# A pace per step for the modulation dots, weights of the seven-product stage split a step ahead

## The chip, the cores and the metric

The kernel runs on one core of a Trainium2 chip. The metric is the device time of one execution in microseconds (us); the time of a kernel is the median of its runs. One execution is also recorded by the hardware profiler, and every row below comes from that one record.

## What is computed

A two-layer encoder over two sequences of 512 tokens (here s0 and s1), width 1024, all in fp32. Layer 0 mixes tokens by bidirectional retention (4 heads), layer 1 by grouped-query attention. Both layers have a squared-ReLU MLP of inner width 4096, and both norms of a layer are modulated: six vectors of 1024 per layer and sequence come from one matrix-vector product with the conditioning vector `c`.

```python
def adaln(c, w, b):
    mod = jax.nn.silu(c) @ w + b            # w: 1024 x 6144
    return [m[:, None, :] for m in jnp.split(mod, 6, axis=-1)]
...
for i in range(DEPTH):
    sh1, sc1, g1, sh2, sc2, g2 = adaln(c, mod_w[i], mod_b[i])
    h = rmsnorm(x, norm1_g[i]) * (1.0 + sc1) + sh1
    m = retention(h, ...) if i % 2 == 0 else attention(h, ...)
    x = x + g1 * m
    h = rmsnorm(x, norm2_g[i]) * (1.0 + sc2) + sh2
    x = x + g2 * (jnp.square(jax.nn.relu(h @ w1)) @ w2)
return rmsnorm(x, final_g)
```

## The kernel before

**Matmuls.** Activations are kept transposed, as eight tiles of 128 features by 512 tokens per sequence. Each fp32 operand is split into a high part (a copy rounded by ACT) and a low part (the difference, taken by DVE), and each product is three matmuls of 128x128 by 128x512 (`mm3`, the lines L220, L221, L222). A weight of the mixers comes as one `raw` tile of 128x1024 on SP's queue; `load_piece` splits it into `whi` (ACT, L207) and `wlo` (DVE, L208). One such piece feeds 24 matmuls.

**Stages in order of time.** The head (to 43 us); retention in eight steps, one head of one sequence each (s0 in steps 0 to 3, s1 in steps 4 to 7, to about 927 us); the entry of the MLP stage of layer 0, with s0's last up projections (`ups`) before and after the pools are changed at about 952 us; its seven-product part (1024 to 1530); the last down projections; attention (1576 to 1985); the same MLP stage for layer 1; the final norm. A retention step runs `scores`, `v` (four pieces), `g` (one piece), `y`, an interleaved list of pieces for the next step's queries and keys and this step's other gates (`ORDER`), and `out`. Step 3 also carries the first norm of s1, step 7 the second norm of s0: the sum of squares is multiplied out on PE, a chain of small DVE operations on 128x4 values (L271, L237 to L244) takes the root, DVE lays it on a diagonal (L275), PE spreads that (`spread`, L281), and DVE and ACT modulate eight tiles (L290, L293; in the MLP stages L312, L315).

**Modulation as background work.** After the first chunks, the modulation product runs on DVE: one task reads a 128x1024 block of `modw`, as two tiles loaded from POOL's queue (L409), and makes two `dot` instructions (L384, an elementwise product with a running sum) for each sequence: four, or two where a chunk is for s1 only. `mod_chunk` queues eight tasks for each chunk. `tick` is called at every mixer piece, behind its `wlo`: it adds `pace[0]` to a credit, and when the credit reaches 1 it issues the dots of one task and asks for the loads of the next. So a pace above 1 still gives one task a piece, and the rest of the credit is kept. `bg_until` and `flush` issue tasks down to a count at given points. The tiles of a task come from the pool `f2`, where one pair is free beside the conditioning and rotary tables; a chunk with `alt` takes every second pair from the pool `xfp` instead, so that two tasks' loads can be under way. Without it one load is under way at a time.

**The seven-product stage.** `wide_stage` closes the mixer's pools and opens its own: `sf` (forms), `su` (sums), `sq` (raw weights `rawq` of 128x1024 and their split halves `wh`). It finishes s0's down projections, s1's norm and s1's first up and down projections with these tiles, each weight loaded, split (L227 on ACT, L228 on DVE) and used in one call, while `h_forms` and `h_fetch` build the activations' forms (DVE L732 to L735 and L228). Then `wide_mlp` multiplies two-by-two blocks by seven products (`seven`, L668 to L670). The forms of the hidden activations are parked in DRAM, fetched back from POOL's queue (`fetch_form`), and split by a `cut` (ACT L816, DVE). `after` queues a cut behind the fetch with a count of three products (`late`).

**What sets the order.** Each engine runs its own instructions in the order in which the scheduler puts them, which follows the program's order and its dependencies. A tile that takes the place of one that is still read waits for the reader, and a pool opened over closed ones waits for the tiles that lay there.

## Time and profile before

| | us |
|---|---|
| Median of 3 runs | 2625.1 (2623.26 to 2627.22) |
| Profiled execution | 2615.62 |
| Its span | 2613.8 |
| PE busy | 2518.2 (96%) |
| DVE busy | 1992.3 (76%) |
| ACT busy | 1119.3 (43%) |
| POOL busy | 522.2 (20%) |

PE is the engine that almost never rests; the other three are meant to feed it. The time that a change of order can give or take is therefore what PE lacks of its own steady pace, stall by stall: its idle time, and the stretches after an idle time in which its granted clock is the lower of the two levels.

### The profile page before, as it was taken

To read this page: it belongs to the slowest core of one execution; us is meant where nothing else is said; L and a number is where in the kernel's file an instruction comes from. 1 tells how busy PE (TensorE), PEld (TensorE's weight loads), DVE (VectorE), ACT (ScalarE), POOL (GpSimd) and SP (SyncE) were. 2 spreads that over 40 slices of the span, in tenths; PEclk is the share of its full clock that TensorE was granted. 3 is DMA by queue.
4 is the path that set the end of the run, shared out by engine and by line. 5 is a ranking of instruction groups with operands and counts; after the bars stand their busy time and mean duration, and the time that the engine had idled before them with its cause. 6 is when DMAs were issued, how large, how long until landed. Compare 5 with 4: busy or idle time off the path is not lost. (4 is left out here: it accounts for less than half of the span.)

```text
span 2613.8 us, 32647 instructions
## 1 busy us (share of the span) xinstructions
PE 2518.2 (96%) x11186; PEld 2052.8 (79%) x11186; DVE 1992.3 (76%) x3800; ACT 1119.3 (43%) x1949; POOL 522.2 (20%) x947
## 2 busy tenths in 40 slices
PE   6999998899999999999999999899999999999998
PEld 4878886677888787888788887688788788878887
DVE  7777687879889877676778876877767766688877
ACT  3433233223323444444533344776764444454432
POOL 2312212331221212221421110000114122142100
PEclk9999999999999999999999999999999999999999
DMA  7544445655455655544654444123257444475433
GB/s 251 188 152 147 156 146 163 200 168 165 142 169 162 196 163 196 173 148 159 225 185 131 145 138 125 57 65 94 93 157 275 159 158 161 149 270 164 140 95 105
DMA packets 133994, 414.00 MB, mean 158 GB/s; under 512 B 21250, under 2 KB 24194, under 8 KB 133828
## 3 DMA queue, kind: packets, MB, share of 16 engines
q0 software_dynamic: 68352, 224.58, 25.7%
q1 hardware_dynamic: 59284, 180.32, 22.1%
q10 hardware_dynamic: 6192, 7.02, 0.8%
q8 instruction: 88, 1.44, 0.2%
q14 instruction: 78, 0.64, 0.1%
HBM read 332.15 MB, written 79.69 MB: 158 GB/s over the span
## 5 line engine op out<-in xcount | busy, mean ns | idle before, releaser
L207 ACT ACTIVATE whi<-raw 128x1024 fp32r<-128x1024 f32 x174 | 183.8, 1058 | 332.2 <-PE pm L221 106.3
L220 PE MATMUL pm<-r,whi 128*128 128x512 f32 x768 | 304.2, 399 | 13.3 <-ACT r L1180 5.8
L221 PE MATMUL pm<-r,whi 128*128 128x512 f32 x768 | 302.9, 394 | 4.9 <-DVE r L315 2.4
L222 PE MATMUL pm<-r,wlo 128*128 128x512 f32 x768 | 301.2, 393 | 0.5 <-DVE wlo L208 0.5
L208 DVE TENSOR_TENSOR wlo<-raw,whi 128x1024 fp32r<-128x1024 f32 x174 | 214.6, 1234 | 94.3 <-ACT whi L207 93.7
L227 ACT ACTIVATE wh<-rawq 128x512 fp32r<-128x512 f32 x228 | 142.5, 629 | 291.8 <-PE pm L669 160.7
L227 ACT ACTIVATE wh<-sum 128x512 fp32r<-128x512 f32 x208 | 129.8, 629 | 280.0 <-PE pa L669 176.5
L668 PE MATMUL pa<-r,wh 128*128 128x512 f32 x624 | 242.8, 389 | 0.0
L670 PE MATMUL pa<-r,wh 128*128 128x512 f32 x624 | 242.8, 389 | 0.0
L669 PE MATMUL pa<-r,wh 128*128 128x512 f32 x624 | 242.7, 389 | 0.0
L384 DVE SCALAR_TENSOR_TENSOR junk<-f,f 128x512 bf16<-128x512 f32 x280 | 194.3, 694 | 52.1 <-DMA f<-in_modw_dram 49.2
L409 POOL DMA_DIRECT2D f<-in_modw_dram x168 | 90.7, 540 | 474.5 <-DVE junk L384 378.2
L220 PEld LDWEIGHTS pm<-r,whi 128*128 128x128 f32 x768 | 145.9, 190 | 48.3 <-ACT r L1180 6.2
L668 PE MATMUL pm<-r,wh 128*128 128x512 f32 x468 | 182.9, 391 | 0.9 <-ACT wh L227 0.9
L669 PE MATMUL pm<-r,wh 128*128 128x512 f32 x468 | 182.2, 389 | 0.0
L670 PE MATMUL pm<-r,wh 128*128 128x512 f32 x468 | 182.1, 389 | 0.0
L220 PE MATMUL pa<-whi,r 128*128 128x512 f32 x440 | 174.4, 399 | 5.5 <-ACT whi L207 4.2
L221 PEld LDWEIGHTS pm<-r,whi 128*128 128x128 f32 x768 | 146.3, 190 | 38.2 <-DVE r L293 4.3
L228 DVE TENSOR_TENSOR wh<-sum,wh 128x512 fp32r<-128x512 f32 x208 | 141.6, 686 | 44.9 <-ACT wh L227 43.4
L221 PE MATMUL pa<-wlo,r 128*128 128x512 f32 x440 | 174.8, 397 | 0.6 <-DVE wlo L208 0.6
L222 PE MATMUL pa<-whi,r 128*128 128x512 f32 x440 | 174.1, 396 | 0.0
L222 PEld LDWEIGHTS pm<-r,wlo 128*128 128x128 f32 x768 | 146.0, 190 | 31.9 <-DVE wlo L208 1.2
(277 smaller groups left out, 6040.5 us busy)
## 6 DMA issues: line engine op xcount, KB each, us to landing
rawq<-in_w_dram SPq DMA_DIRECT2D x144, 512.0 KB, 3.8
raw<-in_wri_dram SPq DMA_DIRECT2D x92, 512.0 KB, 3.7
f<-in_modw_dram POOLq DMA_DIRECT2D x168, 256.0 KB, 3.5
r<-hhpark POOLq DMA_DIRECT2D x142, 256.0 KB, 4.2
hhpark<-f POOLq DMA_DIRECT2D x96, 256.0 KB, 2.9
hhpark<-p POOLq DMA_DIRECT2D x88, 256.0 KB, 2.3
raw<-in_wro_dram SPq DMA_DIRECT2D x32, 512.0 KB, 4.2
xf<-park POOLq DMA_DIRECT2D x48, 256.0 KB, 3.2
```

What stands on the lines that cost most here:

```text
L207: act(hi, raw, AF.Copy)
L208: ins = tt(lo, raw, hi.bitcast(F32), ALU.subtract)
L220: mm(ps, a[0], b[0], start=first, stop=False)
L221: mm(ps, a[0], b[1], start=False, stop=False)
L222: return mm(ps, a[1], b[0], start=False, stop=last)
L227: split.last = act(hi, src_f32, AF.Copy)
L228: split.dve = tt(lo, src_f32, hi.bitcast(F32), ALU.subtract)
L384: stt(junk, w[hf], 0.5, cb[hf], ALU.mult, ALU.mult, accum_out=a[:, 2 * k + hf:2 * k + hf + 1])
L409: nc.gpsimd.dma_start(hv[hf], modw[layer, ch * KD + k][:, hf * T:(hf + 1) * T])
L668: mm(ps, a[0], b[0], start=first and k == 0, stop=False, **more)
L669: mm(ps, a[0], b[1], start=False, stop=False, **more)
L670: mm(ps, a[1], b[0], start=False, stop=k == n - 1, **more)
```

## The change

Four edits, with no arithmetic changed.

1. `PACE` becomes seven numbers, set at the end of the inner part of steps 0 to 6, where one number, 0.88, was set after step 0. From this the tasks per phase follow: in step 2's `out` one for three, in step 3's `v` two for four, in its `ORDER` part two for seven; in steps 4 to 6 sixteen per step for fourteen, one at every piece; in step 7 fewer in the gates, and the last two tasks are issued by the `flush` behind the last `ups`, where none were left before. The chunks 1, 0, 2 and 5 of layer 0 and chunk 4 of layer 1 get `alt`.
2. `late` counts four products for three: each cut of forms is issued one product later.
3. In the entry of `wide_stage` the weights of the next step are loaded and split before the matmuls of the present one are issued.
4. Pools: `wh` and `rawq` get a pool each, `wh` first, so that `rawq` now lies at a higher address, over tiles of the pool `f2` (among them the conditioning tiles that the dots read); after the stage the mixers' pools are opened with `rawp` ahead of `xfp` and `wp`.

```diff
-PACE = 0.88
+PACE = (0.9, 0.9, 0.3, 1.1, 1.1, 1.1, 0.4)
...
     def rawtile():
-        return sq["p"].tile([P, 1024], F32, tag="raw", name="rawq", bufs=SQ_RAW)
+        return sq["p"].tile([P, 1024], F32, tag="raw", name="rawq")
...
     def wtile():
-        return sq["p"].tile([P, T], F32R, tag="w", name="wh", bufs=SQ_W)
+        return sq["w"].tile([P, T], F32R, tag="w", name="wh")
...
-            late.append([3, cut])
+            late.append([4, cut])
...
-        sq["p"] = wide_pools.enter_context(tc.tile_pool(name="sq", bufs=1, reuse_waits="tile"))
+        sq["w"] = wide_pools.enter_context(tc.tile_pool(name="wh", bufs=SQ_W, reuse_waits="tile"))
+        sq["p"] = wide_pools.enter_context(tc.tile_pool(name="sq", bufs=SQ_RAW, reuse_waits="tile"))
...
-        d = m.downs(0, 0, lambda o: nc.gpsimd.dma_start(park[0][o], m.x[0][o]))
-        run(d, 1)
-        nm.a()
-        run(d, 1)
-        nm.c()
-        nm.m(4)
...
+        steps = ([("d", 0, i) for i in range(4)] + [("u", 1, f) for f in range(4)]
+                 + [("d", 1, i) for i in range(4)])
+        load = lambda q: m.w1(0, q[2]) if q[0] == "u" else m.w2(0, q[2])
...
+        w = load(steps[0])
+        for n, (kind, s, i) in enumerate(steps):
+            nxt = load(steps[n + 1]) if n + 1 < len(steps) else None
+            if kind == "u":
+                if i == 0:
+                    m.hh[s] = []
+                m.up(w, s)
+            else:
+                m.down(w, i, s, lambda o, s=s: nc.gpsimd.dma_start(park[s][o], m.x[s][o]))
+            w = nxt
+            for f in hand_over.get(n, ()):
+                f()
...
-                mod_chunk(cb, 0, 1, (1,))
-                mod_chunk(cb, 0, 0, (1,))
-                mod_chunk(cb, 0, 2, (1,))
+                for ch in (1, 0, 2):
+                    mod_chunk(cb, 0, ch, (1,), True)
                 for ch in (4, 3, 5):
-                    mod_chunk(cb, 0, ch)
+                    mod_chunk(cb, 0, ch, alt=ch == 5)
                 for ch in (1, 0, 2, 3, 4, 5):
-                    mod_chunk(cb, 1, ch, alt=ch < 4)
-                pace[0] = PACE
+                    mod_chunk(cb, 1, ch, alt=ch < 5)
+            if step < 7:
+                pace[0] = PACE[step]
...
-    xfp, wp, rawp = mixer_pools(reuse_waits="tile")
+    rawp, xfp, wp = mixer_pools(("rawp", "xfp", "wp"), reuse_waits="tile")
```

Lines of the changed kernel are one higher than before, up to the seven-product part.

On DVE in step 3, from the sum of squares of s1's norm (L271) on; `junk<-f,f` are dots, `s` the small values, `r<-pa,r` the low halves of the values. Before:

```order
L271 TENSOR_SCALAR s_3685<-pm 128x4
L384 SCALAR_TENSOR_TENSOR junk,s_1407<-f_3636,f_923 128x512
L237 TENSOR_SCALAR s_3687<-s_3685 128x4
L208 TENSOR_TENSOR wlo<-raw,whi 128x1024
L228 TENSOR_TENSOR r<-pa,r 128x512
L238 TENSOR_TENSOR s_3688<-s_3687 128x4
L384 SCALAR_TENSOR_TENSOR junk,s_1407<-f_3637,f_928 128x512
L239 SCALAR_TENSOR_TENSOR s_3688<-s_3688,s_3685 128x4
L240 SCALAR_TENSOR_TENSOR s_3687<-s_3688,s_3687 128x4
L384 SCALAR_TENSOR_TENSOR junk,s_1406<-f_3714,f_162 128x512
L241 TENSOR_TENSOR s_3688<-s_3687 128x4
L242 SCALAR_TENSOR_TENSOR s_3688<-s_3688,s_3685 128x4
```

After:

```order
L272 TENSOR_SCALAR s_3631<-pm 128x4
L385 SCALAR_TENSOR_TENSOR junk,s_1403<-f_3583,f_928 128x512
L238 TENSOR_SCALAR s_3633<-s_3631 128x4
L209 TENSOR_TENSOR wlo<-raw,whi 128x1024
L229 TENSOR_TENSOR r<-pa,r 128x512
L239 TENSOR_TENSOR s_3634<-s_3633 128x4
L240 SCALAR_TENSOR_TENSOR s_3634<-s_3634,s_3631 128x4
L241 SCALAR_TENSOR_TENSOR s_3633<-s_3634,s_3633 128x4
L242 TENSOR_TENSOR s_3634<-s_3633 128x4
L243 SCALAR_TENSOR_TENSOR s_3634<-s_3634,s_3631 128x4
L244 SCALAR_TENSOR_TENSOR s_3635<-s_3634 128x4
L245 SCALAR_TENSOR_TENSOR s_3633<-s_3635,s_3633 128x4
```

Three dots stood between the sum of squares and the last root operations shown; one is left, and none stands in the rest of the chain.

On DVE at the entry of layer 0's MLP stage; `p<-pm` and `f<-f` belong to the last pieces of `out` (the new values and their squares), `wh<-rawq` are the splits of the first weights of the stage, `junk` are dots, and `mc_5` and `ng` close the last modulation vector of layer 1. Before:

```order
L263 TENSOR_TENSOR f<-f 128x512
L588 SCALAR_TENSOR_TENSOR p<-pm,mc_2_1_1401,p 128x512
L228 TENSOR_TENSOR wh<-rawq,wh 128x512 x2
L263 TENSOR_TENSOR f<-f 128x512
L228 TENSOR_TENSOR wh<-rawq,wh 128x512
L588 SCALAR_TENSOR_TENSOR p<-pm,mc_2_1_1401,p 128x512
L228 TENSOR_TENSOR wh<-rawq,wh 128x512
L263 TENSOR_TENSOR f<-f 128x512
L588 SCALAR_TENSOR_TENSOR p<-pm,mc_2_1_1401,p 128x512
L263 TENSOR_TENSOR f<-f 128x512
```

After (L610 is the last `ups`):

```order
L385 SCALAR_TENSOR_TENSOR junk,s_1435<-f_8390,f_923 128x512
L392 TENSOR_TENSOR mc_5_0_1436<-s_1434,mb_sb 128x8
L385 SCALAR_TENSOR_TENSOR junk,s_1435<-f_8391,f_928 128x512
L393 TENSOR_TENSOR mc_5_0_1436<-mc_5_0_1436,s_1434 128x8
L392 TENSOR_TENSOR mc_5_1_1437<-s_1435,mb_sb 128x8
L856 TENSOR_SCALAR ng_0_17989<-mc_5_0_1436 128x8
L393 TENSOR_TENSOR mc_5_1_1437<-mc_5_1_1437,s_1435 128x8
L856 TENSOR_SCALAR ng_1_17991<-mc_5_1_1437 128x8
L610 SCALAR_TENSOR_TENSOR f<-pm,f 128x512
L229 TENSOR_TENSOR wh<-rawq,wh 128x512 x2
L229 TENSOR_TENSOR r<-f,r 128x512
L229 TENSOR_TENSOR wh<-rawq,wh 128x512 x2
```

The last task's dots moved to here from earlier, and the splits of the first weights of the stage moved from among the pieces of `out` to behind the last `ups`. The first `rawq` tile of the stage lies where `f_928` and its neighbours lay, and its load on SP waits for the last dot above.

On ACT in the seven-product part of layer 0, where the products of the up units end and those of the down units begin; `sf<-sf` and `r<-r` are the cuts, `wh<-sum` the weights of the next products. Before:

```order
L227 ACTIVATE wh<-rawq 128x512 x2
L816 ACTIVATE sf<-sf 128x512 x3
L780 ACTIVATE f<-pa 128x512
L816 ACTIVATE sf<-sf 128x512 x4
L816 ACTIVATE r<-r 128x512 x5
L227 ACTIVATE wh<-sum 128x512
L788 ACTIVATE f<-pa 128x512
L789 ACTIVATE p<-f 128x512
L227 ACTIVATE wh<-sum 128x512 x3
```

After:

```order
L228 ACTIVATE wh<-rawq 128x512 x2
L817 ACTIVATE sf<-sf 128x512 x2
L781 ACTIVATE f<-pa 128x512
L817 ACTIVATE sf<-sf 128x512 x5
L817 ACTIVATE r<-r 128x512
L228 ACTIVATE wh<-sum 128x512
L817 ACTIVATE r<-r 128x512 x3
L789 ACTIVATE f<-pa 128x512
L817 ACTIVATE r<-r 128x512
L790 ACTIVATE p<-f 128x512
L228 ACTIVATE wh<-sum 128x512 x2
```

Between the last `wh<-rawq` and the first `wh<-sum` behind it twelve cuts stood, and eight stand now; three of the other four come behind that `wh<-sum`, the fourth behind an eviction.

## Rows read from the trace of the kernel before

**Rows 1.** The page, part 1: busy us, share of span, instructions.

```profile
PE 2518.2 (96%) x11186; PEld 2052.8 (79%) x11186; DVE 1992.3 (76%) x3800; ACT 1119.3 (43%) x1949; POOL 522.2 (20%) x947
```

**Rows 2.** Timeline of PE, 410 to 428 us: start, length, instruction [idle before, releaser].

```profile
409.68 0.39 PE L221 MATMUL pm<-r,whi 128*128 128x512 f32 x1
...
412.62 0.39 PE L222 MATMUL pm<-r,wlo 128*128 128x512 f32 x1
415.24 0.50 PE L220 MATMUL pa<-r 128*128 128x512 f32 x1 [2.23 <-DVE r L228]
...
422.39 2.07 PE L281 MATMUL pm<-f,ones 128*128 128x512 f32 x2 [5.95 <-DVE f L275]
...
425.11 0.63 PE L220 MATMUL pa<-r 128*128 128x512 f32 x1
...
427.25 0.63 PE L222 MATMUL pa<-r 128*128 128x512 f32 x1
```

**Rows 3.** Stretches: length, busy us per engine (instructions), granted clock, DMA share, GB/s.

```profile
386.00:518.00 132.00, 115.57 (x473) 89.33 (x473) 102.81 (x228) 41.06 (x58) 37.78 (x66) 0.92 0.54 174
518.00:630.00 112.00, 106.61 (x473) 86.70 (x472) 95.52 (x219) 33.01 (x43) 26.49 (x43) 1.00 0.54 167
630.00:733.00 103.00, 103.00 (x463) 85.35 (x464) 93.55 (x203) 31.93 (x42) 21.99 (x38) 1.00 0.54 163
841.00:947.00 106.00, 101.30 (x446) 82.69 (x445) 88.21 (x192) 49.28 (x74) 18.78 (x35) 0.98 0.54 168
```

**Rows 4.** The same view, stretches around seven stalls of PE.

```profile
412.60:428.60 16.00, 7.82 (x19) 4.94 (x18) 12.28 (x33) 2.14 (x3) 1.61 (x3) 0.68 0.47 148
486.00:500.40 14.40, 10.30 (x26) 6.43 (x25) 11.83 (x25) 1.99 (x3) 4.11 (x9) 0.64 0.58 188
1010.00:1020.00 10.00, 6.55 (x21) 4.51 (x20) 10.00 (x18) 5.28 (x10) 1.61 (x3) 0.83 0.32 124
1296.20:1305.80 9.60, 5.46 (x14) 3.56 (x12) 8.73 (x15) 8.81 (x17) 7.00 (x14) 0.64 0.89 309
1575.50:1589.00 13.50, 8.73 (x22) 6.10 (x21) 10.72 (x17) 6.15 (x8) 1.08 (x2) 0.62 0.48 156
2034.00:2044.00 10.00, 6.56 (x21) 4.23 (x20) 10.00 (x18) 4.60 (x9) 1.08 (x2) 0.83 0.28 89
2319.00:2330.00 11.00, 7.86 (x21) 5.53 (x20) 8.97 (x15) 9.36 (x18) 7.53 (x15) 0.69 0.93 320
```

**Rows 5.** Timeline of DVE, 404 to 424 us.

```profile
416.30 0.15 DVE L271 TENSOR_SCALAR s<-pm 128x4 f32<-128x4 f32 x1
```

**Rows 6.** Waits of DVE, first 518 to 557, then 573 to 930 us.

```profile
DVE junk L384 <- DMA f<-in_modw_dram: 10.7, 6, 3.7
...
DVE junk L384 <- DMA f<-in_modw_dram: 6.0, 6, 1.4
```

**Rows 7.** The page, part 5: busy us, mean ns | idle before, releaser.

```profile
L384 DVE SCALAR_TENSOR_TENSOR junk<-f,f 128x512 bf16<-128x512 f32 x280 | 194.3, 694 | 52.1 <-DMA f<-in_modw_dram 49.2
```

**Rows 8.** The page, part 6: issues, KB each, median us to landing.

```profile
f<-in_modw_dram POOLq DMA_DIRECT2D x168, 256.0 KB, 3.5
```

**Rows 9.** Timeline of SP, 920 to 950 us.

```profile
926.89 13.53 SPq L67 DMA_DIRECT2D rawq<-in_w_dram  x5
```

**Rows 10.** Timeline of PE, 944 to 953 us.

```profile
951.77 0.39 PE L220 MATMUL pm<-r,wh 128*128 128x512 f32 x1
```

**Rows 11.** Tile rawq, 920 to 1000 us.

```profile
DMA to landing us min/median/max: 3.7/4.4/7.5
```

**Rows 12.** Timeline of PE, 1010 to 1020 us.

```profile
1015.11 0.53 PE L222 MATMUL pm<-r,wh 128*128 128x512 f32 x1 [2.80 <-DVE wh L228]
```

**Rows 13.** Timeline of ACT, 1285 to 1302 us.

```profile
1295.95 1.18 ACT L816 ACTIVATE sf<-sf 128x512 fp32r<-128x512 f32 x2 [1.61 <-DMA sf<-hhpark]
...
1299.64 0.61 ACT L227 ACTIVATE wh<-sum 128x512 fp32r<-128x512 f32 x1
```

**Rows 14.** Timeline of PE, 1294 to 1306 us.

```profile
1300.31 0.79 PE L668 MATMUL pa<-sf,wh 128*128 128x512 f32 x1 [3.70 <-ACT wh L227]
```

More of the change, by code (lines that the diff above doesn't have):

```diff
@@ L79, with mixer_pools @@
     mixer = ExitStack()
-    def mixer_pools(**kw):
-        return [mixer.enter_context(tc.tile_pool(name=n, bufs=b, **kw)) for n, b in (("xfp", 3), ("wp", 4), ("rawp", 2))]
-    xfp, wp, rawp = mixer_pools()
+    def mixer_pools(names, **kw):
+        bufs = {"xfp": 3, "wp": 4, "rawp": 2}
+        return [mixer.enter_context(tc.tile_pool(name=n, bufs=bufs[n], **kw)) for n in names]
+    xfp, wp, rawp = mixer_pools(("xfp", "wp", "rawp"))
     dp = mixer.enter_context(tc.tile_pool(name="dp", bufs=1))
@@ L909, in wide_stage @@
         wide.negate()
-        d = m.downs(0, 0, lambda o: nc.gpsimd.dma_start(park[0][o], m.x[0][o]))
-        run(d, 1)
-        nm.a()
-        run(d, 1)
-        nm.c()
-        nm.m(4)
-        run(d, 1)
-        nm.m()
-        run(d)
-        wide.h_fetch(0)
-        m.ups(0, 1, [0])
-        wide.h_fetch(1)
-        m.ups(0, 1, [1])
-        wide.h_forms(0)
-        m.ups(0, 1, [2])
-        wide.h_fetch(2)
-        m.ups(0, 1, [3])
-        wide.h_forms(1)
-        d = m.downs(0, 1, lambda o: nc.gpsimd.dma_start(park[1][o], m.x[1][o]))
-        run(d, 1)
-        wide.h_fetch(3)
-        wide.h_forms(2)
-        run(d, 1)
-        wide.h_forms(3)
-        run(d)
+        steps = ([("d", 0, i) for i in range(4)] + [("u", 1, f) for f in range(4)]
+                 + [("d", 1, i) for i in range(4)])
+        load = lambda q: m.w1(0, q[2]) if q[0] == "u" else m.w2(0, q[2])
+        hand_over = {0: [nm.a], 1: [nm.c, lambda: nm.m(4)], 2: [nm.m], 3: [lambda: wide.h_fetch(0)],
+                     4: [lambda: wide.h_fetch(1)], 5: [lambda: wide.h_forms(0)], 6: [lambda: wide.h_fetch(2)],
+                     7: [lambda: wide.h_forms(1)], 8: [lambda: wide.h_fetch(3), lambda: wide.h_forms(2)],
+                     9: [lambda: wide.h_forms(3)]}
+        w = load(steps[0])
[10 more added lines that the diff above has]
+                f()
         wide_mlp(wide, m)
```

## The prediction

> **What bounds the kernel now.** I read the page first: PE is busy 96% of the span [rows 1], so the question is where the rest is, and who causes it. Next the timeline of PE: unhindered, 13 starts take 2.94 us (409.68 to 412.62), 0.226 us each; after the idle of 5.95 us the starts from 425.11 to 427.25 are 0.43 us apart, which is the lower of the two clock levels, while the idle of 2.23 us before 415.24 was followed by a short matmul again [rows 2]. Then the stretches: with 0.227 us for each matmul, a stretch's length minus count times 0.227 is what PE lost in it, idle and slow clock together. Over whole retention steps [rows 3]: 386 to 518 lost 132 - 473 x 0.227 = 24.6 us, 518 to 630 lost 4.6, 630 to 733 nothing (a few matmuls are shorter, hence -2.1), 841 to 947 lost 4.7. Around single stalls [rows 4]: 11.7 and 8.5 (both inside the 24.6), 5.2 at 1010, 6.4 at 1296, 8.5 at 1575, 5.2 at 2034 and 6.2 at 2319. So some 65 us of loss lie in places that the change touches, each a wait of PE for DVE or ACT, made dearer by the clock behind it.
>
> **Step 3, the norm and the dots (pace).** Today the sum of squares reaches DVE at 416.30 [rows 5] and PE gets the diagonal at 422.39 [rows 2]: 6.1 us of chain, in which DVE also does three dots, 0.69 us each [rows 7]. The dots ahead of it had also waited for their loads. In the new order one dot is left in the chain, PE's `spread` stands behind the 24 matmuls of the gate piece (5.4 us), and the modulates behind it have no dots between them. The chain without two dots, and without the wait of its last one, is about 6.1 - 1.8 = 4.3 us, with the low halves ahead of it 1.9 more, so PE waits some 1 us instead of 5.95 and stays at the full clock. The loss at 486 to 500 has the same root: DVE, busy 102.8 us of 132, works off dots ahead of the evictions. I take 21 of the 24.6 us back; the bounds are 13 (only the stall at 412 and little else) and 24.
>
> **Steps 4 to 6, more dots.** Sixteen tasks for fourteen, in each of three steps: two tasks are eight dots of 0.69 us, 5.6 us more of DVE per step. From the two rows, DVE goes from 93.6 to 99 of 103 us and from 95.5 to 101 of 112 [rows 3]: it still fits, but with 4 us of room where nothing was lost before. For it speaks that the waits for loads shrink: 10.7 us in six waits at 518 to 557, where one load at a time was under way, against 6.0 in six over the whole of 573 to 930, where most chunks had two pairs [rows 6]; nearly all chunks have two now. I take 2 us lost, with bounds of 10 lost (a wait of 0.2 us of PE at each of 48 pieces) and 3 won (most of the 4.6 at 518). Steps 1 and 2 change from 0.88 to 0.9 of a task a piece: nothing, within 2 us.
>
> **Step 7.** Its norm keeps five dots for eight in the chain, and one task for two stands between the modulates: 2 us of the 4.7 lost, bounds 0 and 4.
>
> **Entry of layer 0's MLP stage (pools and the last tasks).** Now SP issues five `rawq` loads from 926.89 on [rows 9], and PE goes from the last `ups` to the first `wh` without a gap, at 951.77 [rows 10]. After the change the first of these loads lies over tiles that the dots read, and waits for the last dot, which stands behind the last piece of `out` and next to the last `ups`: by the pieces of `out`, 2.7 us apart, about 951. The other loads and the splits on ACT and DVE are queued behind it. A `rawq` load lands in 4.4 us here, 3.7 to 7.5 [rows 11], and the split adds some 0.6, so PE has its first `wh` at about 956, 4 us after it ran out, and pays some 3.5 us of lower clock after that, by what the stall at 412 lost, 11.7, less its two idles of 2.23 and 5.95 [rows 2, 4]. I take 8 us lost, bounds 4 and 12. This is a new wait, not one moved.
>
> **The prelude of both MLP stages (weights a step ahead).** The stall at 1010 is PE waiting 2.80 us for a `wh` low half [rows 12], which DVE does behind the form operations of the step; asked for a step earlier, it stands ahead of them in the order. The operations are the same in number, and DVE was busy 10.0 of 10.0 us there [rows 4], so what is saved for PE comes due for the forms, which nothing needs until the seven products begin. I take 5 of the 5.2 in layer 0, bounds 2 and 6, and 4.5 of the 5.2 in layer 1 [rows 4], bounds 2 and 5; the entry of layer 1 has no dots to wait for.
>
> **Cuts one product later.** ACT cuts at 1295.95 what has just landed, and reaches the `wh<-sum` that PE waits for at 1299.64, seven cuts later [rows 13]; PE idles 3.70 us [rows 14]. With four cuts fewer ahead of it, at 3.69 us for seven, that `wh` comes 2.1 us earlier: the idle falls to 1.6. The next `wh<-sum` then has the four cuts, an eviction and a square ahead of it, and makes PE wait 1 us more after the first product. Whether the clock falls on the sum of both is open: if it stays, 6.4 becomes 2.8; if it falls, 5.2. I take 3 us won here and 3 at the twin (6.2) [rows 4], bounds 0.5 and 4 each.
>
> **Attention.** The second mixer pools have `rawp` at another address, so the first loads of `wai` start earlier, but DVE's order there is the same, and the low half stays behind the modulates: 1 of the 8.5 us [rows 4], bounds 0 and 3.
>
> **The sum.** 21 - 2 + 2 - 8 + 5 + 4.5 + 3 + 3 + 1 = 29.5 us won. The profiled execution took 2615.6 us, 9.5 below the median of the runs; the terms are differences, so I take them from the median: 2625.1 - 29.5 = 2595.6, say 2596.
>
> **Rivals.**
>
> DVE becomes the bound (slower than before). Should each of the 48 tasks in steps 4 to 6 wait for its load, DVE's room of about 5 us a step is used up first, and the rest delays every eviction that PE needs: 48 x w - 15 us for a mean wait of w. The other terms win 31.5, so it is slower than before from w = 0.97 us on. The six waits at 518 to 557 were 1.8 each, which would give 2625.1 - 31.5 + 48 x 1.8 - 15 = 2665; w = 1.2 gives 2636. Against it stand six waits of 1.0 in the whole of 573 to 930 [rows 6], some 40 tasks, so 0.15 a task, and a landing of 3.5 us [rows 8] against a piece of 5.4.
>
> The Trainium skill, page "SBUF — State Buffer", section "SBUF: two separate sides", speaks for this rival: a DMA issued from GpSimd needs its descriptors written by GpSimd, which a DVE operation that holds the shared port pair locks out, so that a DMA of 620 ns alone took 3100 beside such an operation. The dots' loads are issued there, and a fuller DVE would by that rule delay the loads it waits for. The trace does not bear this out so far: the waits fell where DVE was busiest.
>
> The change does not do what it says at the entry. Waiting for the last dot puts the whole chain of weights back; SP's other loads follow it, the tiles are three, and the split a step ahead finds its weights late through the prelude. Then layer 0's 5 us are not won and the entry costs 12: 29.5 - 9 = 20.5, 2605. For it speaks that the first load here can take 7.5 us [rows 11], against it that five loads fit in 13.5 us of SP [rows 9] when nothing holds them.
>
> The waits only move. The dots taken from step 3's middle are the same dots; if evictions in `out` or the modulates wait instead, step 3 gives 13, the cuts 0.5 each, and 2625.1 - 29.5 + 8 + 5 gives 2609.
>
> Full relief. The last dots end earlier than I think, or the loads come faster, so that the entry costs 2; the cuts give 4 each, step 3 gives 24: 29.5 + 6 + 2 + 3 = 40.5, 2585.
>
> **How the numbers follow.** Forecast 0.55, entry 0.15, waits only move 0.13, full relief 0.10, DVE the bound 0.07. The range of 2576 to 2614 takes in the first four with the bounds of their terms (all upper bounds together, 24 + 3 + 2 + 4 - 4 + 6 + 5 + 4 + 4 + 3 = 51, would give 2574, and not all will meet), and leaves out DVE's case and a little of the tails. About 0.2% (5 us) is what a measurement of this kernel can tell from no change. Faster by more: the first four cases, less the lower ends of the third, 0.88. Within 0.2%: 0.06, from those ends and the mild end of DVE's case. Slower: 0.06.
>
> **What the profile afterwards would show.** Step 3 right: the wait for the diagonal near 1 us and the stretch of that step some 20 us shorter at a granted clock near 1.00. Steps 4 to 6 right: DVE near 95% of the stretch and waits for `in_modw` well under 1 us a task; wrong: those waits at the head of PE's. Entry: a first PE idle of 4 us on a `wh<-rawq` near the change of stage, and the load's issue right behind the last dot; no such idle, and my reading of the addresses is wrong. Prelude: no wait for `wh` L229 at the counterparts of 1010 and 2034. Cuts: an idle under 2 us in place of 3.70, then one near 1; a low clock behind them would take half the gain. The prediction is wrong as a whole if the time of steps 4 to 6 grows by more than 10 us, or if step 3 keeps more than half of its 24.6.

## The result, and the profile after

| | before | after |
|---|---|---|
| Median of the runs, us | 2624.2 (2622.3 to 2627.2, 4 runs) | 2590.3 (2586.1 to 2592.1, 4 runs) |
| Ratio | | 0.987, 95% interval 0.985 to 0.9885 |
| Profiled execution's span, us | 2613.8 | 2590.3 |

The change makes the kernel 34 us faster; the interval allows 30 to 39. The two recorded spans differ by 23.5 us only. The record of before is 9 us below the median of its own runs, that of after 2 us above, and the experiments below show where part of that lies.

The view of stretches of the changed kernel, for steps 3 to 6 and for step 7 up to the end of the last up projections but one; columns as in [rows 3]: length, busy us of each engine with its instructions (the first pair is PE's), granted clock, share of the DMA engines, GB/s.

```profile
380.00:498.00 118.00, 112.07 (x492) 91.19 (x491) 91.25 (x178) 42.07 (x59) 32.84 (x55) 0.98 0.54 171
498.00:611.00 113.00, 109.42 (x477) 89.30 (x476) 97.20 (x227) 31.81 (x42) 26.35 (x45) 0.98 0.54 168
611.00:714.00 103.00, 103.00 (x464) 85.36 (x463) 97.16 (x221) 32.12 (x42) 25.90 (x42) 1.00 0.56 173
714.00:819.00 105.00, 105.00 (x472) 87.03 (x472) 96.21 (x219) 32.06 (x42) 26.06 (x44) 1.00 0.56 174
819.00:932.00 113.00, 106.85 (x464) 86.95 (x464) 92.18 (x204) 48.17 (x71) 21.46 (x40) 0.97 0.49 151
```

With 0.227 us for each of PE's matmuls, as in the prediction, PE lost 118 - 492 x 0.227 = 6.3 us in step 3, where it lost 24.6 before, 4.7 in step 4 (4.6 before), nothing in steps 5 and 6, and 7.7 in step 7, where it lost 4.7 [rows 3]. DVE is busy 97 of 103 us in step 5, as the sum said.

The same view around the stalls that answer to [rows 4], with one stretch that is new (1975 to 1992):

```profile
488.00:500.40 12.40, 7.90 (x23) 5.62 (x22) 7.28 (x14) 2.01 (x3) 5.39 (x11) 0.72 0.90 269
932.80:944.00 11.20, 4.39 (x14) 3.17 (x13) 4.09 (x9) 3.31 (x6) 0.00 (x0) 0.70 0.86 298
995.00:1005.00 10.00, 9.79 (x44) 7.78 (x43) 10.00 (x17) 3.98 (x7) 2.17 (x4) 1.00 0.53 154
1277.00:1286.60 9.60, 8.53 (x37) 6.44 (x36) 8.91 (x16) 7.23 (x15) 4.98 (x10) 1.00 1.01 379
1554.50:1568.00 13.50, 7.82 (x22) 5.57 (x21) 10.65 (x17) 6.16 (x8) 1.08 (x2) 0.75 0.46 160
1975.00:1992.00 17.00, 15.05 (x57) 11.22 (x56) 13.08 (x21) 10.50 (x18) 8.66 (x17) 0.90 0.87 311
2014.50:2024.50 10.00, 9.80 (x43) 7.78 (x42) 10.00 (x18) 3.98 (x7) 2.17 (x4) 1.00 0.54 164
2297.00:2308.00 11.00, 10.27 (x46) 7.91 (x45) 10.41 (x18) 9.66 (x19) 7.64 (x15) 1.00 0.96 346
```

Losses by the same arithmetic: 7.2 us at 488 to 500, which is a new place (see below); 8.0 at the entry of layer 0's MLP stage (nothing before); nothing at 995 to 1005 (5.2); 1.2 at 1277 (6.4); 8.5 at 1554, as before to the tenth; 4.1 at 1975 (nothing before); 0.2 at 2014 (5.2); 0.6 at 2297 (6.2). The norm's stall of 11.7 us is gone as a whole: two waits for evictions, of 0.9 and 0.5 us, are what PE has left between 412 and 488.

PE runs the same 11186 matmuls in both kernels, in the same order but for a few exchanges, so a place can also be found in both traces by the matmul that stands there. By this the stall of 8.5 us at 486 of before, early in `out`, where PE waits for evictions,

```profile
490.98 0.79 PE L220 MATMUL pm<-r,whi 128*128 128x512 f32 x1 [1.74 <-DVE p L588]
```

is gone as a whole too: the same matmuls run from 468 to 482 after the change and lose nothing. The loss at 488 to 500 lies some 80 matmuls later, behind `out`, where step 4's scores begin, and there the kernel before lost 13 - 51 x 0.227 = 1.4 us. After, and before:

```profile
468.00:482.00 14.00, 14.00 (x63) 11.58 (x63) 12.13 (x23) 2.26 (x4) 4.31 (x8) 1.00 0.59 197
```


```profile
511.00:524.00 13.00, 11.72 (x51) 9.05 (x50) 10.17 (x18) 5.60 (x7) 4.29 (x8) 1.00 0.84 283
```

The new stall at the entry, in the timelines of DVE, SP and ACT (start, length, instruction, idle time before it and what ended it):

```profile
931.88 0.69 DVE L385 SCALAR_TENSOR_TENSOR junk<-f,f 128x512 bf16<-128x512 f32 x1
...
932.61 16.62 SPq L67 DMA_DIRECT2D rawq<-in_w_dram  x6
...
939.52 1.15 ACT L228 ACTIVATE wh<-rawq 128x512 fp32r<-128x512 f32 x2 [5.44 <-DMA rawq<-in_w_dram]
```

and in that of PE:

```profile
940.21 0.79 PE L221 MATMUL pm<-r,wh 128*128 128x512 f32 x1 [6.81 <-ACT wh L228]
```

The last dot runs from 931.88 to 932.57, the first of the raw loads is issued at 932.61, ACT splits it at 939.52 when it has landed, and PE, which ran out at 933.4, goes on at 940.21. This is the chain that the order of instructions and the addresses announced.

The new loss behind step 3, in the timeline of DVE (a dot that waits for its load, and the eviction behind it) and of PE:

```profile
492.39 0.69 DVE L385 SCALAR_TENSOR_TENSOR junk<-f,f 128x512 bf16<-128x512 f32 x1 [2.80 <-DMA f<-in_modw_dram]
...
493.00 0.75 DVE L589 SCALAR_TENSOR_TENSOR p<-pm,mc,p 128x512 f32<-128x512 f32 x1
```


```profile
493.81 0.79 PE L221 MATMUL pm<-r 128*128 128x512 f32 x1 [4.50 <-DVE p L589]
```

DVE stands 2.80 us before a dot whose load is late, and the eviction `p` (L589), which PE waits for, is behind that dot in DVE's row. PE idles 4.50 us and runs at the lower clock after it (granted 0.72 over the stretch). The load was late for two reasons. Its issue stood on POOL's queue behind a fetch of s1's tile, which waited 3.00 us for a parking to land, until 486.99; and the two loads issued behind that took 4.9 us to land, against the 3.5 of [rows 8] (the view of DMA issues as there, 487 to 489 us):

```profile
f<-in_modw_dram POOLq DMA_DIRECT2D x2, 256.0 KB, 4.9
```

The DMA engines were busy 0.90 of that stretch, and 0.54 of the whole step.

### The profile page after: what moved, and what is told of

Same layout as the page of the kernel before. It is cut to its first block, busy times and chain, and to the rows that moved or that the text cites. A ratio compares the mean times of both kernels' runs of the same rounds, so it can differ in the third digit from the quotient of the medians.

```text
span 2590.3 us, 32585 instructions
## 1 busy us (share of the span) xinstructions
PE 2505.1 (97%) x11186; PEld 2048.7 (79%) x11186; DVE 1993.7 (77%) x3800; ACT 1119.1 (43%) x1949; POOL 525.2 (20%) x947
## 4 chain that ended last, share of the span: by engine, by line
PE 67%; issue 12%; DVE 9%; DMA 6%; POOL 4%; ACT 1%; POOLq 0%; SPq 0%; ACTq 0%; DVEq 0%
PE pm L222 6%; PE pm L223 6%; PE pm L221 6%; PE pa L671 6%; PE pa L669 6%; PE pa L670 6%; PE pa L222 5%; PE pa L223 5%; PE pa L221 5%; PE pm L671 4%; PE pm L670 4%; PE pm L669 4%; DVE junk L385 2%; POOL hhpark L761 1%; DMA f<-in_modw_dram 1%
## 5 line engine op out<-in xcount | busy, mean ns | idle before, releaser
L221 PE MATMUL pm<-r,whi 128*128 128x512 f32 x768 | 302.8, 397 | 11.7 <-ACT r L1176 5.8
L223 PE MATMUL pm<-r,wlo 128*128 128x512 f32 x768 | 300.3, 391 | 0.0
L223 PE MATMUL pa<-whi,r 128*128 128x512 f32 x440 | 174.1, 396 | 0.0
L385 DVE SCALAR_TENSOR_TENSOR junk<-f,f 128x512 bf16<-128x512 f32 x224 | 156.4, 698 | 22.3 <-DMA f<-in_modw_dram 19.3
L229 DVE TENSOR_TENSOR wh<-rawq,wh 128x512 fp32r<-128x512 f32 x228 | 155.2, 683 | 21.8 <-ACT wh L228 21.5
L223 PEld LDWEIGHTS pm<-r,wlo 128*128 128x128 f32 x768 | 145.0, 189 | 30.4
```

The source lines that it names most:

```text
L221: mm(ps, a[0], b[0], start=first, stop=False)
L223: return mm(ps, a[1], b[0], start=False, stop=last)
L229: split.dve = tt(lo, src_f32, hi.bitcast(F32), ALU.subtract)
L385: stt(junk, w[hf], 0.5, cb[hf], ALU.mult, ALU.mult, accum_out=a[:, 2 * k + hf:2 * k + hf + 1])
```

## The experiments

Each ran beside the kernel before on the same chip, and the ratios below are to those runs of before, whose medians were 2624.6, 2622.0, 2623.7 and, for the last experiment, 2626.5 us.

### One edit at a time

**The pace alone.** To the kernel before:

```diff
-PACE = 0.88
+PACE = (0.9, 0.9, 0.3, 1.1, 1.1, 1.1, 0.4)
...
+            if step < 7:
+                pace[0] = PACE[step]
```

(with the `alt` of the change)

> The kernel before with the first edit alone (a pace per step, and the chunks with two tile pairs). Theory: the edits add up by place, and the pace's places are the retention steps. The trace after lost 9.8 us in step 3 where 25.3 were lost before, 2.8 less in steps 1 and 2, some 2 less in steps 4 to 6, and 3.4 more in step 7: 17 us won, about 2607 us, and no stall of PE at the entry of layer 0's MLP stage, since the raw weights lie at their old place; the last dots only keep DVE busy there. Rival: the two last tasks behind the last up projections cost the entry by themselves, because the splits of the first weights stand behind them on DVE; then some 4 to 8 us of the 17 are gone (2611 to 2615) and PE waits for a low half at the entry.

Measured: 2601.7 us, ratio 0.9919 (0.9906 to 0.9931), 21 us faster. That is more than the 17 of the theory, while the two records differ by 11.7 only: the record of before lies 9 us below its median (see below) and this one 2 above. At the entry PE waits a little, for ACT:

```profile
936.75 0.50 PE L220 MATMUL pm<-r,wh 128*128 128x512 f32 x1 [1.65 <-ACT wh L227]
```

So the two tasks behind the last up projections cost 2.3 us there with the pools in the old order, 1.65 of it in this wait, and not 8. The theory had no stall of PE there and the rival 4 to 8 us: it lies between, nearer to the theory.

**The cuts alone.**

```diff
-            late.append([3, cut])
+            late.append([4, cut])
```

> The kernel before with the second edit alone (each cut of forms one product later). Theory: the loss at the change from up to down units falls from 6.8 to about 1.6 us in layer 0 and from 6.6 to about 1.0 in layer 1, and two small waits at 1380 and 1457 go with it: 11 to 12 us won, about 2613. Rival, my prediction's term: 3 us each, since a second wait comes after the first product and the clock may fall: about 2618. Other rival: the gain there came from the pools or the weights ahead, and this edit alone gives nothing.

Measured: 2610.8 us, ratio 0.9955 (0.9941 to 0.9968), 12 us by the ratio, 14 by the medians. The stretches of the two counterparts of 1296 and 2319:

```profile
1303.00:1312.00 9.00, 8.20 (x35) 5.93 (x34) 9.00 (x16) 8.48 (x17) 6.54 (x14) 1.00 0.98 360
2317.00:2326.00 9.00, 8.25 (x35) 6.12 (x34) 8.82 (x15) 8.93 (x18) 6.31 (x12) 1.00 0.97 363
```

9 - 35 x 0.227 = 1.1 us lost in each, at the full clock, for 6.4 and 6.2 before. The wait behind the first product that I feared is not there, and the clock does not fall. The theory holds, the prediction's 3 + 3 was half of it.

**The weights a step ahead alone.** The `steps` loop of the diff in the kernel before.

> The kernel before with the third edit alone (weights of the MLP stage's entry split a step ahead, old pools, old pace). Theory: layer 0's prelude wins the 7 us lost at 995 and 1010 to 1020, and gives 2.8 back at the first products, as in the trace after; layer 1 the same: 5.8 lost before at 2034, 3.2 after, 2.6 won, 6 to 7 us in all, about 2618. The trace after also had a new loss of 4.3 us at 1983 to 1991 in layer 1 (PE waiting for the modulated tiles). Rival A: it comes from this edit, because one more split stands ahead of the modulates on DVE: then it is here too, and the edit wins only 2 us. Rival B: it comes from the pools or from timing, and isn't here.

Measured: 2617.0 us, ratio 0.9976 (0.9965 to 0.9987), 6.3 us faster. The stretches at 1012 and 2032 answer to 1010 and 2034 of before, the one between them is the change from up to down units, where this edit does nothing:

```profile
1012.00:1022.00 10.00, 9.80 (x43) 7.78 (x43) 10.00 (x18) 4.56 (x8) 2.04 (x4) 1.00 0.54 184
1297.50:1309.50 12.00, 8.10 (x23) 5.76 (x22) 9.79 (x17) 10.37 (x20) 8.16 (x16) 0.72 0.88 305
2032.00:2042.00 10.00, 9.78 (x44) 7.78 (x43) 10.00 (x17) 4.43 (x8) 2.17 (x4) 1.00 0.57 182
```

Nothing is lost in the prelude (10 - 43 x 0.227 = 0.2 and 10 - 44 x 0.227 = 0), where 5.2 each were; 6.8 us are still lost at 1297, so the cuts' gain is the cuts' own. At layer 1's modulates PE lost 0.7 us, not 4.3: rival A falls. What the edit gives back are two waits at the first seven-product weights in each layer, of 1.24 and 0.99 us, which were not there before (2.8 us with what PE loses around them).

This run and the one before it leave the code of the retention steps as it was, and so show how far that place varies. DVE's wait for the dots' loads in its first 40 us, in this kernel:

```profile
DVE junk L384 <- DMA f<-in_modw_dram: 12.5, 7, 3.7
```

It was 10.7 in [rows 6], and PE lost 65 - 236 x 0.227 = 11.4 us of the stretch 500 to 565 here against 5.8 in the record of before (65 us, 261 matmuls). That record was a mild one: against this run some 5 of its 9 us below the median lie in this place, and less against the next run, which also leaves this code alone.

**The pools alone.**

```diff
+        sq["w"] = wide_pools.enter_context(tc.tile_pool(name="wh", bufs=SQ_W, ...))
+        sq["p"] = wide_pools.enter_context(tc.tile_pool(name="sq", bufs=SQ_RAW, ...))
...
-    xfp, wp, rawp = mixer_pools(reuse_waits="tile")
+    rawp, xfp, wp = mixer_pools(("rawp", "xfp", "wp"), reuse_waits="tile")
```

> The kernel before with the fourth edit alone (the pools of the MLP stage and of attention in the new order, old pace). Theory: by itself it wins nothing: no dots are left at the end of step 7, so the first load of raw weights waits for older dots only, and the attention's start keeps its 8.9 us; within 2 us of before. Rival: the first load at the entry waits for the conditioning tiles' last reader also here, at about 909 us, which is before it is issued now (927): no loss. Other rival: the new place costs layer 1's entry the 4.3 us at the modulates: 4 us slower.

Measured: 2626.3 us, ratio 1.0012 (1.0003 to 1.0021), 3 us slower. No stall at layer 0's entry, 8.0 lost at the start of attention as ever, and layer 1's entry lost 3.6 us at the modulates: the other rival. Step 4 is at its harsher end here too:

```profile
DVE junk L385 <- DMA f<-in_modw_dram: 12.4, 6, 3.8
```

The four edits by their ratios: 21.3 + 11.8 + 6.3 - 3.1 = 36 us, against 35 for the change (0.9867). The pools are the part that loses.

### Which pools, and what each costs

**The changed kernel with the old MLP pools.**

```diff
-        sq["w"] = wide_pools.enter_context(tc.tile_pool(name="wh", bufs=SQ_W, ...))
-        sq["p"] = wide_pools.enter_context(tc.tile_pool(name="sq", bufs=SQ_RAW, ...))
+        sq["p"] = wide_pools.enter_context(tc.tile_pool(name="sq", bufs=1, reuse_waits="tile"))
```

> The changed kernel with the MLP stage's old pools (one pool, raw weights at the lower address), all else as changed. Theory: the stall of 8.4 us at the entry of layer 0's MLP stage comes from the pace and the pools together, since the pools alone showed none and the pace alone showed 2.3: it falls to about 2.3. And the 4.3 us at layer 1's modulates (1983 to 1991), which the pools alone showed too (3.6), go with the place of the raw weights: together 10 us, about 2580. Rival A: layer 1's loss belongs to the order of the mixers' pools, not to these: 2584. Rival B: the weights asked for a step ahead wait at the entry for something else that is late: 2590.

Measured: 2589.4 us, ratio 0.9878 (0.9864 to 0.9893): no gain. The stretch of layer 0's entry and that of layer 1's modulates:

```profile
934.50:945.70 11.20, 9.85 (x46) 7.63 (x46) 7.50 (x21) 4.35 (x8) 1.09 (x2) 1.00 0.88 343
1975.00:1990.00 15.00, 12.26 (x37) 7.85 (x36) 13.08 (x22) 11.05 (x18) 9.37 (x18) 0.77 0.76 254
```

PE idles 1.28 us at the entry instead of 6.81, and by its matmuls some 2 us are lost of the 8 (the arithmetic on the stretch gives 0.8, but eight of its matmuls are the norm's short ones): that half of the theory holds. But layer 1's modulates lost 15 - 37 x 0.227 = 6.6 us instead of 4.1, layer 1's entry another 2.6 (a wait for ACT's split at 1952), and the cuts there 4.2 instead of 1.0. The first two come again in the other kernel with this pair of pools (below), the 3 us at the cuts do not, so they are not the pools'. Under the mixers' new order the old MLP pools are the worse ones for layer 1. What the entry gave, layer 1 took, and the 10 us that I added up fell.

**The changed kernel with the mixers' pools in the old order.**

```diff
-    rawp, xfp, wp = mixer_pools(("rawp", "xfp", "wp"), reuse_waits="tile")
+    xfp, wp, rawp = mixer_pools(reuse_waits="tile")
```

> The changed kernel with the mixers' pools opened in the old order for attention. Theory: that order does nothing that can be measured: the attention's start keeps its 8.9 us, since the low half on DVE stands behind the modulates either way; 2590 within 2. Rival: the earlier raw loads of attention are what delays layer 1's entry, and its 4.3 us go: 2585.

Measured: 2585.9 us, ratio 0.986 (0.9844 to 0.9877), against 0.9867 (0.985 to 0.9885) for the change: the intervals overlap, so by time alone it is not told apart. In the trace it is: the stretch of layer 1's modulates lost nothing here (17 - 76 x 0.227 is below zero), where the changed kernel lost 4.1.

```profile
1975.00:1992.00 17.00, 17.00 (x76) 13.77 (x75) 14.62 (x23) 12.93 (x22) 9.21 (x18) 1.00 0.95 345
```

By the trace the theory falls, and the rival's 4.3 us go; that attention's earlier raw loads make them, as the rival had it, no run separates. What the trace shows: the third of DVE's modulates in the changed kernel waits for a parking transfer,

```profile
1978.36 0.75 DVE L313 SCALAR_TENSOR_TENSOR f<-p,mc,f 128x512 f32<-128x512 f32 x1 [2.49 <-DMA park<-f]
```

and POOL's queue, which issues that parking, first fetches s1's tiles. In the changed kernel those fetches wait, one of them for PE (L223), and the last four are issued from 1968.42 to 1970.80:

```profile
1963.00 0.54 POOL L250 DMA_DIRECT2D p<-park  x1 [1.13 <-PE pm L223]
...
1968.42 2.38 POOL L250 DMA_DIRECT2D p<-park  x4 [0.98 <-DMA f<-park]
```

With the old order the last five go from 1965.02 to 1968.17:

```profile
1965.02 3.15 POOL L249 DMA_DIRECT2D p<-park  x5 [0.70 <-DMA f<-park]
```

Why a fetched tile has to wait for PE longer there I did not take apart; that the mixers' order decides it is shown, by this pair and by another below. The start of attention lost 7.5 to 8.9 us in all these kernels, with either order.

**The changed kernel without its pool edits.** Both diffs above undone, three edits kept.

> The changed kernel without its fourth edit: old pools in both places, the other three edits kept. Theory: with the old MLP pools the entry of layer 0 lost 1.9 us instead of 8.4, but layer 1's entry and its cuts lost 9 more with the new order of the mixers' pools; with the mixers' old order and the new MLP pools layer 1's entry lost nothing, and the entry of layer 0 kept its stall. So the two pool edits were needed for each other, and without both the trace loses about 6.5 less at layer 0's entry and 4 to 5 less at layer 1's: 2579. Rival: the cut one product later leans on the place of the new MLP pools; then layer 1's cuts lose 3 us again: 2582. Other rival: the sum of the three edits alone, 22.9 + 13.8 + 7.6 = 44 us off 2624: 2580, which is the same number by another way.

Measured: 2583.1 us, ratio 0.9855 (0.9838 to 0.9871), 3 us more than the change won by the ratios and 7 by the medians, with overlapping intervals. Layer 1's entry and cuts were clean (nothing at the modulates, 1.0 at the cuts: the rival on the cuts falls), and 4.1 us were lost at layer 0's entry, where the timeline of PE shows an odd price for a short wait:

```profile
935.09 0.50 PE L220 MATMUL pm<-r,wh 128*128 128x512 f32 x1 [1.84 <-ACT wh L227]
...
937.52 0.63 PE L220 MATMUL pm<-r,wh 128*128 128x512 f32 x1
937.94 0.63 PE L221 MATMUL pm<-r,wh 128*128 128x512 f32 x1
```

An idle of 1.84 us, and then matmuls 0.42 us apart, the lower clock.

**No task behind the last up projections.** The kernel without pool edits, and

```diff
-PACE = (0.9, 0.9, 0.3, 1.1, 1.1, 1.1, 0.4)
+PACE = (0.9, 0.9, 0.3, 1.1, 1.1, 1.1, 0.6)
```

> The run before with the last pace 0.6 for 0.4, so that no task is left behind the last up projections. Theory: the 1.9 us left at layer 0's entry go too, step 7's norm costs the same: 2 to 3 us faster than the run before, 2576. Rival: the dots moved into step 7 cost what they save: the same.

Measured: 2578.3 us, ratio 0.9829 (0.9815 to 0.9842). The entry, for which the run before lost 4.1 us, lost 11.2 - 49 x 0.227 = 0.1:

```profile
938.00:949.20 11.20, 11.20 (x49) 8.88 (x49) 9.40 (x22) 4.83 (x9) 2.35 (x5) 1.00 0.51 168
```

The same step was taken with only the MLP pools put back:

> As the run before (old MLP pools), and the last pace 0.6 for 0.4, so that no task is left behind the last up projections; two more tasks run in step 7's gates and ups. Theory: the 2.3 us left at the entry go, and step 7's middle pays nothing, since its norm has the same tasks ahead of it: about 2578. Rival: the two tasks fall on the modulates of step 7 (3.4 us lost there already) and cost as much as they save: the same as the run before within 2 us, or 2 us slower.

Measured: 2586.7 us, ratio 0.9865 (0.985 to 0.988). The entry lost nothing here either, and layer 1 kept its 7 us at the modulates. The 2578 was counted from the 2580 expected of the kernel that this one starts from, which came at 2589.4. Both gained 3 to 5 us by the last pace, a little more than expected, though the intervals overlap with those of the kernels that they start from. And these two kernels differ by the order of the mixers' pools alone: with the old MLP pools that order is told apart by time as well, 0.9829 against 0.9865, with intervals that don't meet.

### The dots and their loads

**The second tile pair for the same chunks as before.** The changed kernel, and

```diff
-                    mod_chunk(cb, 0, ch, (1,), True)
+                    mod_chunk(cb, 0, ch, (1,))
...
-                    mod_chunk(cb, 0, ch, alt=ch == 5)
+                    mod_chunk(cb, 0, ch)
...
-                    mod_chunk(cb, 1, ch, alt=ch < 5)
+                    mod_chunk(cb, 1, ch, alt=ch < 4)
```

> The changed kernel with the second tile pair given to the same chunks as before only (chunks 1, 0, 2, 5 of layer 0 and 4 of layer 1 have one pair again). Theory: the waits of DVE for the dots' loads come back where these chunks run, from 19 us to 40 or 50 in sum, and PE loses 5 to 12 us more, mostly in steps 3 to 5 and 7: about 2598. Rival: the pace alone keeps the dots out of PE's way, and the waits lie in DVE's slack: within 3 us of 2590. My rival from the prediction, DVE as the bound, would show here as a slower steps 4 to 6 by over 10 us.

Measured: 2596.6 us, ratio 0.9905 (0.989 to 0.992): 6 to 10 us of the change's gain are gone. DVE's waits for the dots' loads from 43 to 940 us (sum, times, longest), in the changed kernel:

```profile
DVE junk L385 <- DMA f<-in_modw_dram: 19.3, 16, 2.9
```

and without the second pairs:

```profile
DVE junk L385 <- DMA f<-in_modw_dram: 35.6, 32, 2.8
```

With the waits for the tiles of the second pool (`xf`) it is 22.1 and 37.1: the theory holds, with waits a little shorter than it said. From the first matmul of step 4's scores to that of step 5's PE took 125.5 us, 119.0 with the pairs, and the other steps up to 6 were the same within 0.6. So the pairs are part of why sixteen tasks fit; without them the waits grow by two thirds, and still they are far from making DVE the bound.

**More dots early.** The kernel without pool edits, and

```diff
-PACE = (0.9, 0.9, 0.3, 1.1, 1.1, 1.1, 0.4)
+PACE = (1.1, 1.1, 0.3, 1.1, 1.1, 1.1, 0.5)
...
                 pace[0] = PACE[step]
+                if step in (2, 6):
+                    pace[1] = 0.0
```

> Old pools, and the paces 1.1, 1.1, 0.3, 1.1, 1.1, 1.1, 0.5 with the credit set to zero at the end of steps 2 and 6: more dots in steps 1 and 2, where DVE was busy 75 to 81 of 108 us, so that out of step 3 runs a chunk with two tile pairs and step 7 has six tasks for eleven. Theory: the two losses that are left in the retention steps are dots that wait for their loads in step 3's out (7.5 us) and dots in step 7's norm and modulates (9 to 10 us); with fewer dots there half of both goes: 2570. Rival: the dots put into steps 1 and 2, where chunk 4 of layer 0 has one pair, make their own waits for loads there, and PE loses 4 to 8 us in steps 1 and 2: 2576 or more.

Measured: 2575.8 us, ratio 0.982 (0.9807 to 0.9834), with steps 1 and 2 as long as in the changed kernel (105.2 and 105.4 us between the scores, 105.2 and 105.2 there), so their DVE had the room: the rival's reason falls. The theory's 2570 is missed all the same. Step 7 lost 116 - 499 x 0.227 = 2.7 us where the changed kernel lost 7.7:

```profile
805.00:921.00 116.00, 113.20 (x499) 92.28 (x498) 94.81 (x200) 49.53 (x72) 21.53 (x41) 0.99 0.51 160
```

But the place behind step 3's `out` lost 10.6, more than ever. The edit did not do there what I expected of it: all dots from 440 to 515 us read `f`, so the chunk in `out` was still one with a single pair, and the first dot on a second pair (`xf`) comes at 516. DVE and POOL, timelines:

```profile
496.52 0.69 DVE L384 SCALAR_TENSOR_TENSOR junk<-f,f 128x512 bf16<-128x512 f32 x1 [6.66 <-DMA f<-in_modw_dram]
```


```profile
485.63 0.54 POOL L249 DMA_DIRECT2D p<-in_xs_dram  x1 [5.06 <-DMA park<-p]
487.20 0.54 POOL L249 DMA_DIRECT2D p<-in_xs_dram  x1 [1.03 <-DMA park<-p]
...
488.53 1.06 POOL L409 DMA_DIRECT2D f<-in_modw_dram  x2 [0.25 <-issue]
```

A dot waits 6.66 us for its load. On POOL's queue the fetches of s1's tiles (L249, into the tiles that were just parked) wait 5.06 and 1.03 us for the parking to land, and the two loads of the dots, issued at 488.53, come behind them. But the dots that read these tiles last had ended at 486.6 and 487.3, so the queue cost these loads under 2 us. The larger part is the transfer: they landed 7.9 and 8.8 us after their issue, against a median of 3.5 [rows 8]. The same view, 488.2 to 489.4 us:

```profile
f<-in_modw_dram POOLq DMA_DIRECT2D x2, 256.0 KB, 8.3
```

That the parkings and fetches beside them on the DMA engines make it so slow is likely, but no run separates it. Nor did any run put a chunk with two pairs there, so whether a second pair would hide it stays open.

**No dots in step 3's `out`.** The kernel with the last pace 0.6, without pool edits, and

```diff
-PACE = (0.9, 0.9, 0.3, 1.1, 1.1, 1.1, 0.6)
+PACE = (1.1, 1.1, 0.3, 1.1, 1.1, 1.1, 0.6)
...
-                pace[0] = PACE[step]
+                pace[0] = PACE[step] if step != 3 else 0.0
+                if step == 2:
+                    pace[1] = 0.0
...
                 r = r1
+                pace[0] = PACE[3]
```

> Old pools, last pace 0.6, and no task in step 3's out; its four tasks run in steps 1 and 2 instead (pace 1.1 there, credit set to zero at the end of step 2). Theory: the 7 to 10 us that every kernel with the new paces still lost at 488 to 503 come from POOL's queue: in step 3's out it also carries the parking of s0 and the fetches of s1, whose tiles wait for the parking to land, and the dots' loads wait behind these fetches, so DVE stands 3 to 7 us before a dot with PE's evictions behind it. Without dots there the loss falls to 2 or less: 2578 - 6 = 2572, and steps 1 and 2 pay under 2. Rival: the wait there is for the evictions themselves (DVE behind PE's pace in out), then PE still loses 5 us or more at 488 to 503 and the time stays at 2578.

Measured: 2570.0 us, ratio 0.9793 (0.9778 to 0.9807). PE's waits from 380 to 512 us, all of them, and the stretch around the place:

```profile
PE pm L220 <- DVE p L588: 2.6, 1, 2.6
```


```profile
484.00:500.00 16.00, 13.43 (x59) 10.77 (x58) 11.52 (x22) 4.51 (x6) 5.33 (x10) 1.00 0.79 265
```

One wait of 2.6 us is left, 16 - 59 x 0.227 = 2.6 us lost at the full clock, where 7 to 10 were. The theory holds in its number. That the dots hold up the evictions there is shown; by how much the late issue and by how much the slow landing do, is not, since the edit takes out both. Nor is the whole gain from this place: of the 10 us between this record and that of the kernel that it starts from, by the same matmuls, 4 lie here, 4 in the rest of step 4 and 3 in step 7, whose dots the same edit moved. This is the fastest of the kernels, 55 us below the kernel before and 20 below the change.

## Why the prediction was right, and where its sum was off

2596 was forecast, 2590.3 came, inside 2576 to 2614. The sum of 29.5 has errors of both signs, and that the total came so near is in part luck: step 7 and layer 1's entry and prelude came 11.5 us below their terms, the cuts and steps 4 to 6 some 8 above. Against the two recorded executions, term by term (won, in us):

| Step of the sum | forecast | trace |
|---|---|---|
| Step 3 | 21 | 18.3 |
| Steps 4 to 6 | -2 | about 1 |
| Step 7 | 2 | -3 |
| Entry of layer 0's MLP stage | -8 | -8 |
| Prelude, layer 0 | 5 | 4 |
| Cuts, both layers | 3 + 3 | 5.2 + 5.6 |
| Start of attention | 1 | 0 |
| Entry and prelude, layer 1 | 4.5 | -2 |

Smaller places won about 3 (steps 1 and 2, and two short waits of the seven-product part).

**Step 3** went as argued at the norm, and further: PE's `spread` waits for nothing. The stall at 486 went as argued as well: DVE stood idle for no more than 0.4 us there before the change, with dots ahead of evictions, and with fewer dots nothing is lost. What the sum set at nothing is the end of `out`. There a dot now waits for its load, 2.80 us of PE's 4.50, and 7.2 us are lost where 1.4 were; in all the kernels with the new paces and a task left in this `out` it is 7 to 11. My rival of waits that only move named this place, evictions in `out`.

**Steps 4 to 6** held, with DVE at 97 of 103 us. The size was wrong in the other direction from what I feared: the record of before happened to show 10.7 us of waits, other executions of the same code 12.4 to 12.5 with twice the loss of PE. Against those the term is +5 to +7 rather than -2, and this is also part of why the medians differ by 34 and the records by 23.5.

**Step 7** failed. I counted the dots inside the chain, five for eight. The trace has five after the change but six before, so it got shorter by less: 7.7 us from the sum of squares on DVE (848.63) to PE's `spread` (856.34), 8.6 before (868.66 to 877.29). And ahead of the chain stood, beside the three dots and three low halves that stood there before, a `wlo` of 1.2 us: DVE took the sum 5.6 us after PE had begun it (843.07), 4.1 before (864.60). And PE had 15 of `y`'s matmuls ahead of the `spread`, 20 before. So it waited 3.3 us where it had waited 1.6, and after that it ran some 3 us at the lower clock (matmuls 0.43 us apart), which it had not before. For step 3 I had looked at PE's order, for step 7 not.

**The entry** came by the mechanism that I gave: last dot at 931.88, load at 932.61, PE idle 6.8 with 1.2 us of slower matmuls behind. That the price fits to the tenth is luck. I had said 4 idle and 3.5 of clock; the load took 6.9 us from its issue to its split, near the upper end of its row [rows 11], and the clock cost less. The experiments add that it took two of the four edits to make it: either alone cost 2.3 or nothing.

**The prelude** in layer 0 gave what was lost, less 2.8 us of new waits at the first weights of the seven products: I had said that nothing needs the forms until then, and then is when PE waited. In layer 1 the same, and the mixers' pool order took 4.1 us at the modulates. I had costed that edit at the start of attention alone, where it did nothing; what lies under the next stage's pools I did not follow.

**The cuts** were worth twice my term. I put the four cuts behind the `wh` as a second wait of 1 us and left half for the clock; neither came. PE now comes to the second `wh` after twelve matmuls (1286.44) where it came to it after two (1301.97 before), and of the waits that are left the longer, 0.73 us in each layer, ends with a low half on DVE; ACT ends one of 0.34 in layer 0.

**The rivals.** DVE as the bound did not come: waits for loads fell from 49 to 22 us in all. The Trainium skill, page "SBUF — State Buffer", section "SBUF: two separate sides", says that GpSimd cannot write the descriptors of its DMAs while DVE runs an operation in a two-port mode. It does not say this of every DVE operation, as I took it. The median landing of the dots' loads is 3.5 us as in [rows 8], with DVE at 94% of step 5, so no run here shows it for these operations. The loads that did cost time landed late, 4.9 us in the changed kernel and 7.9 and 8.8 in one of the others, and in that one DVE itself stood idle for 6.66 us of it, so a busy DVE is not what held them. The entry cost the forecast's 8 us and not the rival's 12, and the prelude behind it lost nothing. That waits would move came in part: 7 us behind step 3's `out`.

## What to carry to other kernels

A background task that shares a queue with the foreground (here DVE's dots, and their loads on POOL) should be paced by what that queue does in each phase: it was free in steps 1 and 2, and in one `out`, where parkings and fetches take the same queue and the same DMA engines, a dot behind a late load held up PE's evictions in every kernel with the new paces that put one there. The order in which pools are opened is a set of waits between stages: a pace that cost 2 us and an address that cost nothing made an 8 us stall together, and the order chosen for one stage cost 4 us in the next; the stage that follows has to be read too. Before a term is sized from one record, look at whether other executions show the same loss there. And a stall in the trace after is the old one only if the same matmuls wait in it: here one went, and another of nearly the same size came some 80 matmuls later.

## What the runs showed that I had not expected

- The clock after a short idle is not told by its length alone: PE kept the full clock after an idle of 2.57 us in the kernel without dots in `out` (granted 1.00 over the stretch) and ran at the lower level after one of 1.84 us at the entry of the kernel without pool edits (matmuls 0.42 us apart, for some 3.5 us).
- One record of a kernel can lie 9 us from the median of its runs without any disturbance that the profile names: waits for loads of the same code in step 4 were 10.7, 12.4 and 12.5 us, and PE's loss around them 5.8 to 11.4.
